# Gate/value products of a Strassen-Winograd feed-forward in another order

## The chip, the cores and the metric

The kernel runs on one core of a Trainium2 chip. The metric is device time in microseconds (us), the median of repeated executions. TensorE (PE) does the matrix products; VectorE (DVE), ScalarE (ACT) and GpSimd (POOL) do the arithmetic around them; SyncE (SP) and ScalarE issue DMA transfers. Each engine works through its own queue in order.

## The reference

One layer: a gated linear attention mixer, then a feed-forward with a causal convolution over three tokens, in fp32, for 2048 tokens of 1024 features. The part that the change touches is the first half of the feed-forward (FFN_DIM is 2816):

```python
def conv_ffn(h, w_up, conv_w, conv_b, w_down):
    u = causal_dwconv(h @ w_up, conv_w, conv_b)
    g, val = jnp.split(u, 2, axis=-1)
    return (jax.nn.silu(g) * val) @ w_down

x = x + y
h = rmsnorm(x, ffn_norm_w[i])
x = x + conv_ffn(h, ffn_w_up[i], ffn_conv_w[i], ffn_conv_b[i], ffn_w_down[i])
return rmsnorm(x, final_norm_w)
```

## The kernel before

Every large product is a 2x2 block product done with seven products in place of eight (Strassen-Winograd), named p1 to p7. Their operands are sums and differences of blocks: those of the weights are called `uw` here, those of the activations `h_s_p`. Every operand is split into a high and a low half, a cast on ScalarE and a difference on VectorE (`split`, L184 to L187), and each product adds three matmuls for each part (`mm3p`, L177 to L179).

The stages follow one another on TensorE: the mixer's products, the gate/value products (`phase_u`, from 893.7 us to about 1790 us of the span), and the down projection. Within `phase_u` the loops run over two token halves s of 1024 tokens ("passes"), eleven groups g in a pass, and fourteen jobs in a group: each of the seven products for the two tiles f = 2g and 2g + 1 (called f0 and f1 here; in the rows of the program's order, `uw_1_4_p5` is the weight operand of p5 for s = 1, f = 4). A job is twelve 128x512 matmuls into one PSUM bank. In the old order a group runs p1, p5, p6, p7, p4, p2, p3, each for f0 and then f1.

The banks carry partial sums from one product to the next:
- Bank `ua` takes p1, and is copied (c1); p6 is added, and it is copied (c2, L1219); p7 is added, and it is copied (c3, L1315); p4 is added, and it is copied into the tile u (L1322). All four copies are ScalarE's.
- Bank `uc` takes p5; VectorE adds c3 to it for one quarter of the output (L1318); then p3 is added, and VectorE adds c2 to it (L1328).
- Bank `ub` takes p2; VectorE adds c1 (L1310).

A product that adds into a bank waits until the bank's copy or add has been done. From the finished tiles u, `conv` does the convolution (an ACT pass at L1235, two DVE scalar-tensor-tensor passes at L1237, called STTs in the text, and the silu at L1239), and `gated` the product of gate and value (L1244) and the operand sums of the down projection on POOL (`as`, L1258 to L1262), which SyncE stores (L1248 to L1264).

`prep` makes the weight operands five jobs ahead of their products: raw weights are loaded by SyncE (`ur`, L1186), summed by POOL into `us` or in place (L1196 to L1214), and split. Two raw tiles per f are loaded in two parts. In the first pass the activation operands of the second pass are made beside the products, in 28 **operand steps** (`prep_h2`): VectorE takes a difference of two loaded blocks (L828), ScalarE and VectorE split it (`h2p`), and ScalarE's queue issues the store to `hd` (L823), a step late. A planner (`spread`, by estimated time) sets where each step falls in the program, one step per 11 us of its own estimate. `load_op` (L886) loads a 2 MB operand (four loads of 512 KB), three jobs behind its predecessor's last product, between the first pass and the second.

At the end of the gate/value stage `d_early` calls parts of the down projection's preparation, which uses freed slots of the operands.

Of the kernel before, what the change touches and what calls it, by code (L numbers as in the profile page):

```python
# [25 lines left out]
def hybrid_kernel(  # L26
# [45 lines left out]
    Y0, Y1, U0, U1 = 3.0, 2.8, 14.0, 11.0  # L72
# [709 lines left out]
    def blocks(tt, rws):  # L782

        for k in range(2):
# [4 lines left out]
            t = hb2_tile(f"hb2_{tt}_{k}") if tt < TT else cp_tile(f"hb3_{tt}_{k}")  # L789
# [12 lines left out]
    def prep_h2(jj, raw, pair):  # L802
# [13 lines left out]
        def store():  # L816
            while held:
                o, hl = held.pop(0)
                if s == 0:
                    nc.sync.dma_start(hd[s, o, j], f32(hl))  # L820
                else:
                    for i in range(2):
                        nc.scalar.dma_start(hd[s, o, j][:, i, :], f32(hl[i]))  # L823
# [58 lines left out]
    def load_op(s, o):  # L882

        t = uh.tile([P, 2, PAIRS, 512], F32R, tag=o, name=f"h_{s}_{o}", bufs=1)
        for j in range(PAIRS):
            nc.sync.dma_start(f32(t[:, :, j, :]), hd[s, o, j])  # L886
# [287 lines left out]
    def phase_u():  # L1174
        raws, wops, sums, made = {}, {}, {}, {}
        jobs = [(s, g, o, f) for s in range(NS) for g in range(NQ) for o in OPS for f in (2 * g, 2 * g + 1)]
        GJ = 2 * len(OPS)
# [39 lines left out]
        def copied(name, pa):  # L1217
            t = cp_tile(name)
            nc.scalar.copy(t, pa)  # L1219
            return t  # L1220
# [49 lines left out]
        bank = {}  # L1270
        for k, (s, g, o, f) in enumerate(jobs):
            if k % GJ in (2, 7) and k // GJ + 1 < NS * NQ:
                load(k // GJ + 1, int(k % GJ == 7))
            if k > 3:
                ls, lg, lo_, lf = jobs[k - 3]
                if ls + 1 < NS and lg == NQ - 1 and lf % 2 == 1:
                    need(*(f"h2p{jj}" for jj in range(PAIRS, 2 * PAIRS)))
                    load_op(ls + 1, lo_)
            if k == 6:
                while delayed:  # L1280
# [5 lines left out]
                spread(range(PAIRS, 2 * PAIRS), U0, U1, row_tile,  # L1286
                       lambda name: tuple(pools["us"].tile([P, 512], F32R, tag="as", name=f"{name}_{i}", bufs=AB) for i in range(2)))
# [6 lines left out]
            pairs = [((wh[:, kt * P:(kt + 1) * P], wl[:, kt * P:(kt + 1) * P]), (hop[o][0][:, kt], hop[o][1][:, kt])) for kt in range(HK)]  # L1294
            if o == "p1":
                a = bank["a", f] = mm_ps(f"ua_{s}_{f}")
                mm3p(a, pairs)
                made["p1", f] = copied(f"c1_{s}_{f}", a)
            elif o == "p5":
                c = bank["c", f] = aux_ps(f"uc_{s}_{f}")  # L1300
                mm3p(c, pairs)
            elif o == "p6":
                a = bank["a", f]
                mm3p(a, pairs, first=False, more=True)
                made["u2", f] = copied(f"c2_{s}_{f}", a)
            elif o == "p2":
                pb = mm_ps(f"ub_{s}_{f}")
                mm3p(pb, pairs)
                ev, _ = new_u(s, 0, f)
                nc.vector.tensor_add(ev, tiles1(pb), tiles1(made.pop(("p1", f))))  # L1310
            elif o == "p7":
                a = bank["a", f]
                mm3p(a, pairs, first=False, more=True)
                u3 = pools["us"].tile([P, 512], F32, tag="as", name=f"c3_{s}_{f}", bufs=AB)
                nc.scalar.copy(u3, a)  # L1315
                ev, od = new_u(s, 1, f)
                made["ev", f] = ev
                nc.vector.tensor_add(od, tiles1(bank["c", f]), tiles1(u3))  # L1318
            elif o == "p4":
# [3 lines left out]
                conv(s, 1, f)  # L1323
            else:
                c = bank.pop(("c", f))
                mm3p(c, pairs, first=False, more=True)
                _, od = tiles2(made["u", 0, f][:, 2:2 + TS])
                nc.vector.tensor_add(od, tiles1(c), tiles1(made.pop(("u2", f))))  # L1328
                conv(s, 0, f)
                gated(s, f)  # L1330
# [42 lines left out]
    def w_slots(o, q):  # L1373
        if q % 4 == 0:
            wgrp[o] = slots(("p7", "p4", "p3")[q // 4], f"dw_{o}_{q}")
        return wgrp[o][q % 4 * 2:][:2]

    def a_slots(k):
        if k % 4 == 0:
            wgrp["a"] = slots(("p6", "p2")[k // 4 % 2], f"da_{k}")  # L1380
# [31 lines left out]
    def d_early(o):  # L1412

        if o == "p6":
            load_chain()
        elif o == "p7":
            d_load(4)
        elif o == "p4":
            d_prep(2)
        elif o == "p3":  # L1420
# [77 lines left out]
    for n, (o, s) in enumerate(units):  # L1498
        banks = [(mm_ps if n % 2 == 0 else aux_ps)(f"pd_{o}_{s}_{m}") for m in range(PAIRS)]
# [54 lines left out]
```

## Time and profile before

| | |
|---|---|
| median of 3 runs | 2221.0 us (2214.37 to 2228.9) |
| profiled execution | 2224.22 us |
| its span | 2222.5 us |
| PE busy | 2122.4 us (95%) |
| DVE, ACT, POOL busy | 1636.5 (74%), 1107.9 (50%), 733.1 us (33%) |
| mean granted clock of TensorE | 0.986 |
| gate/value stage | 893.7 to about 1790 us |
| DMA | 411.78 MB, mean 185 GB/s |

The span runs from the first to the last instruction of one profiled execution. Busy time is summed per engine; a busy PE is not yet PE at its peak, since the clock that it is granted can fall. In rows of a timeline the first number is the start in us, the second the duration, and a bracket gives the idle time of the engine before it, with what ended it.

### The profile page before, as it was taken

How to read it: one execution, taken by the hardware profiler on the slowest of the kernel's cores; microseconds unless marked ns; L12 is line 12 of the kernel's file. 1: busy time of each engine (PE TensorE's matmuls, PEld its weight loads, DVE VectorE, ACT ScalarE, POOL GpSimd, SP SyncE). 2: the span in 40 equal slices, each digit the busy share in tenths (PEclk: the TensorE clock that was granted, in tenths of full speed). 3: DMA queues.
4: the chain of work that ended last, by engine and by line, in shares of the span. 5: the costliest groups of instructions: out<-in, count | busy, mean ns of one | idle time of the engine just before them, and what ended most of it. 6: DMA issues, size and time to landing. Idle time of an engine off the chain costs nothing.

```text
span 2222.5 us, 29090 instructions
## 1 busy us (share of the span) xinstructions
PE 2122.4 (95%) x9952; PEld 1743.6 (78%) x9952; DVE 1636.5 (74%) x2167; ACT 1107.9 (50%) x2024; POOL 733.1 (33%) x602
## 2 busy tenths in 40 slices
PE   6999999989998999898999999999999999999998
PEld 5888787877887787677887777788888887888886
DVE  8655787789778765488899786897877777457564
ACT  5554755565556676444555453454554443333342
POOL 1000011111111000355566664656555435036100
PEclk9999999999999999999999999999999999999999
DMA  6645684478557889935435348433332468354453
GB/s 210 218 165 182 203 264 157 131 223 299 164 161 235 283 321 352 315 117 174 155 120 193 105 139 288 142 112 102 103 111 85 159 243 289 128 180 152 142 176 113
DMA packets 305125, 411.78 MB, mean 185 GB/s; under 512 B 23742, under 2 KB 160110, under 8 KB 304976
## 3 DMA queue, kind: packets, MB, share of 16 engines
q1 hardware_dynamic: 267440, 346.99, 47.2%
q10 hardware_dynamic: 37536, 62.93, 8.4%
q8 instruction: 78, 1.28, 0.2%
q14 instruction: 71, 0.58, 0.1%
HBM read 266.70 MB, written 143.13 MB: 184 GB/s over the span
## 4 chain that ended last, share of the span: by engine, by line
PE 62%; DVE 14%; DMA 9%; issue 7%; ACT 3%; POOL 3%; SPq 1%; ACTq 0%; DVEq 0%; POOLq 0%
PE ua L177 5%; PE pd_p L178 5%; PE pd_p L179 5%; PE pd_p L177 5%; PE ua L179 5%; PE ua L178 5%; DVE t L1237 4%; PE uc L177 2%; PE uc L179 2%; PE uc L178 2%; PE mp_R L177 2%; PE mp_R L179 2%; PE mp_R L178 2%; PE mp_Y L177 2%; PE mp_Y L179 2%
## 5 line engine op out<-in xcount | busy, mean ns | idle before, releaser
L177 PE MATMUL ua<-h_p,uw_p 128*128 128x512 f32 x704 | 280.2, 398 | 23.6 <-ACT c L1219 23.6
L178 PE MATMUL ua<-h_p,uw_p 128*128 128x512 f32 x704 | 278.6, 396 | 0.0
L179 PE MATMUL ua<-h_p,uw_p 128*128 128x512 f32 x704 | 278.4, 395 | 0.0
L1237 DVE SCALAR_TENSOR_TENSOR t<-u,cw,t 128x1024 f32<-128x1024 f32 x176 | 263.3, 1500 | 8.9 <-ACT t L1235 7.9
L178 PE MATMUL pd_p<-dw_p,da 128*128 128x512 f32 x616 | 240.5, 390 | 3.1 <-DVE da L187 3.1
L179 PE MATMUL pd_p<-dw_p,da 128*128 128x512 f32 x616 | 240.1, 390 | 0.0
L177 PE MATMUL pd_p<-dw_p,da 128*128 128x512 f32 x616 | 240.1, 390 | 0.0
L187 DVE TENSOR_TENSOR uw_p<-ur,uw_p 128x512 fp32r<-128x512 f32 x176 | 168.3, 972 | 58.5 <-ACT uw_p L186 53.3
L187 DVE TENSOR_TENSOR da<-da_p,da 128x512 fp32r<-128x512 f32 x154 | 133.6, 920 | 105.4 <-ACT da L186 105.3
L186 ACT CAST da<-da_p 128x512 fp32r<-128x512 f32 x154 | 85.2, 619 | 208.9 <-PE pd_p L179 153.3
L177 PEld LDWEIGHTS ua<-h_p,uw_p 128*128 128x128 f32 x704 | 134.1, 191 | 57.2 <-ACT c L1219 27.6
L186 ACT CAST uw_p<-us 128x512 fp32r<-128x512 f32 x132 | 82.1, 622 | 165.8 <-POOL us L1199 108.3
L187 DVE TENSOR_TENSOR uw_p<-us,uw_p 128x512 fp32r<-128x512 f32 x132 | 120.4, 921 | 57.6 <-ACT uw_p L186 57.2
L179 PEld LDWEIGHTS ua<-h_p,uw_p 128*128 128x128 f32 x704 | 134.0, 190 | 30.1
L178 PEld LDWEIGHTS ua<-h_p,uw_p 128*128 128x128 f32 x704 | 134.3, 191 | 29.5
L177 PE MATMUL uc<-h_p,uw_p 128*128 128x512 f32 x352 | 138.3, 393 | 1.0 <-DVE t L1237 1.0
L179 PE MATMUL uc<-h_p,uw_p 128*128 128x512 f32 x352 | 138.0, 392 | 0.0
L178 PE MATMUL uc<-h_p,uw_p 128*128 128x512 f32 x352 | 138.0, 392 | 0.0
L178 PEld LDWEIGHTS pd_p<-dw_p,da 128*128 128x128 f32 x616 | 116.0, 188 | 28.0 <-DVE da L187 3.9
L1235 ACT ACTIVATE t<-u,cw 128x1024 f32<-128x1024 f32 x88 | 109.8, 1247 | 51.2 <-DVE u L1328 43.3
L179 PEld LDWEIGHTS pd_p<-dw_p,da 128*128 128x128 f32 x616 | 116.0, 188 | 24.2
L177 PEld LDWEIGHTS pd_p<-dw_p,da 128*128 128x128 f32 x616 | 115.9, 188 | 24.0
(269 smaller groups left out, 5476.2 us busy)
## 6 DMA issues: line engine op xcount, KB each, us to landing
ur<-in_ffn_w_up_dram SPq DMA_DIRECT2D x168, 256.0 KB, 3.7
da_p<-ad_p SPq DMA_DIRECT2D x154, 256.0 KB, 4.1
h_p<-hd_p SPq DMA_DIRECT2D x56, 512.0 KB, 8.1
ad_p<-as_p SPq DMA_DIRECT2D x88, 256.0 KB, 2.7
ad_p<-t SPq DMA_DIRECT2D x66, 256.0 KB, 3.5
x<-in_x_dram SPq DMA_DIRECT2D x32, 512.0 KB, 4.3
ch<-in_ffn_w_down_dram SPq DMA_DIRECT2D x61, 256.0 KB, 4.4
hr_A_p<-h1d_p SPq DMA_DIRECT2D x56, 256.0 KB, 2.7
```

Of the source, the lines that this page charges most:

```text
L177: nc.tensor.matmul(ps_ap, ah, bl, start=(first and i == 0), stop=False, **kw)
L178: nc.tensor.matmul(ps_ap, al, bh, start=False, stop=False, **kw)
L179: nc.tensor.matmul(ps_ap, ah, bh, start=False, stop=(last and i == len(pairs) - 1), **kw)
L186: nc.scalar.copy(hi, src)
L187: nc.vector.tensor_sub(lo, src, f32(hi))
L1235: nc.scalar.activation(t, u[:, 2:2 + TS], AF.Identity, scale=cw[:, 2, c:c + 1], bias=cw[:, 3, c:c + 1])
L1237: nc.vector.scalar_tensor_tensor(t, u[:, k:k + TS], cw[:, k, c:c + 1], t, op0=ALU.mult, op1=ALU.add)
```

## The change

The new order of a group is p1, p5, p6, p2 (each for f0 and f1), then p3 of f0, p7 of f0, p3 of f1, p7 of f1, p4 of f0, p4 of f1.

- Between p6 and p7 of one tile there stand now four or five products, before one.
- p5's bank is copied by ScalarE (c5) right after p5, and p7 is read by VectorE out of bank `ua`, which adds c5 (L1331), in place of the copy c3 and the add of c3 to `uc`. Then p4 is added into `ua`.
- p2 uses a bank of the same set as p5 and p3; the tiles of some copies change their pool.
- `conv` and `gated` of a tile are called one job later (`todo`, `late`).
- The operand steps fall at fixed jobs: at jobs 4, 6 and 8 (counted from 0) of the groups 1 to 10 of the first pass. Their stores are issued by SyncE.
- Raw weights of the next group are loaded at jobs 6 and 9, before at jobs 2 and 7.
- The loads of the second pass's operands follow the new order of products; those of p7 and p4 are issued by ScalarE, the others by SyncE.
- The last row tiles use another pool in an earlier stage, and the down projection takes its slots and banks from other operands.

```diff
-    Y0, Y1, U0, U1 = 3.0, 2.8, 14.0, 11.0
+    Y0, Y1 = 3.0, 2.8
+    H2AT = (4, 6, 8)
+    RAWAT = (6, 9)
...
-                        nc.scalar.dma_start(hd[s, o, j][:, i, :], f32(hl[i]))
+                        nc.sync.dma_start(hd[s, o, j][:, i, :], f32(hl[i]))
...
-        jobs = [(s, g, o, f) for s in range(NS) for g in range(NQ) for o in OPS for f in (2 * g, 2 * g + 1)]
-        GJ = 2 * len(OPS)
+        ORDER = [(o, i) for o in ("p1", "p5", "p6", "p2") for i in range(2)]
+        ORDER += [("p3", 0), ("p7", 0), ("p3", 1), ("p7", 1), ("p4", 0), ("p4", 1)]
+        jobs = [(s, g, o, 2 * g + i) for s in range(NS) for g in range(NQ) for o, i in ORDER]
+        GJ = len(ORDER)
...
-            if k % GJ in (2, 7) and k // GJ + 1 < NS * NQ:
-                load(k // GJ + 1, int(k % GJ == 7))
+            if h2u and k >= GJ and k % GJ in H2AT:
+                h2u.pop(0)()
+                while h2u and len(h2u) % 9 in (0, 1):
+                    h2u.pop(0)()
+            if k % GJ in RAWAT and k // GJ + 1 < NS * NQ:
+                load(k // GJ + 1, RAWAT.index(k % GJ))
...
-                    load_op(ls + 1, lo_)
+                    load_op(ls + 1, lo_, nc.scalar if lo_ in ("p7", "p4") else nc.sync)
...
             elif o == "p5":
                 c = bank["c", f] = aux_ps(f"uc_{s}_{f}")
                 mm3p(c, pairs)
+                made["p5", f] = copied(cp_tile(f"c5_{s}_{f}"), c)
             elif o == "p6":
                 a = bank["a", f]
                 mm3p(a, pairs, first=False, more=True)
-                made["u2", f] = copied(f"c2_{s}_{f}", a)
+                made["u2", f] = copied(out_tile(f"c2_{s}_{f}"), a)
             elif o == "p2":
-                pb = mm_ps(f"ub_{s}_{f}")
+                pb = aux_ps(f"ub_{s}_{f}")
...
+            elif o == "p3":
+                c = bank.pop(("c", f))
+                mm3p(c, pairs, first=False, more=True)
+                nc.vector.tensor_add(made.pop(("od", f)), tiles1(c), tiles1(made.pop(("u2", f))))
+                todo.append(lambda s=s, f=f: conv(s, 0, f))
             elif o == "p7":
                 a = bank["a", f]
                 mm3p(a, pairs, first=False, more=True)
-                u3 = pools["us"].tile([P, 512], F32, tag="as", name=f"c3_{s}_{f}", bufs=AB)
-                nc.scalar.copy(u3, a)
-                ev, od = new_u(s, 1, f)
-                made["ev", f] = ev
-                nc.vector.tensor_add(od, tiles1(bank["c", f]), tiles1(u3))
-            elif o == "p4":
+                made["ev", f], od = new_u(s, 1, f)
+                nc.vector.tensor_add(od, tiles1(a), tiles1(made.pop(("p5", f))))
+            else:
                 a = bank.pop(("a", f))
                 mm3p(a, pairs, first=False, more=True)
                 nc.scalar.copy(made.pop(("ev", f)), tiles1(a))
-                conv(s, 1, f)
-            else:
-                c = bank.pop(("c", f))
-                mm3p(c, pairs, first=False, more=True)
-                _, od = tiles2(made["u", 0, f][:, 2:2 + TS])
-                nc.vector.tensor_add(od, tiles1(c), tiles1(made.pop(("u2", f))))
-                conv(s, 0, f)
-                gated(s, f)
+                todo += [lambda s=s, f=f: conv(s, 1, f), lambda s=s, f=f: gated(s, f)]
+            for fn in late:
+                fn()
```

The change shifts line numbers: in the new kernel the split is at L188 and L189, the copies of p1, p5 and p6 at L1223, the adds of p2, p3 and p7 at L1321, L1325 and L1331, the STT at L1241.

ScalarE's queue around the copies c2, in the second group of the first pass, stands so before (`h2p` is an operand step's pair of halves, `hd` its place in memory):

```order
L186 CAST uw_0_2_p2_10133<-ur_0_2_1_9846 128x512
L186 CAST h2p_4_p5_0_10085<-h2r_4_0_9942 128x512
L823 DMA hd_1_p5_0_318<-h2p_4_p5_0_10085 128x512
L823 DMA hd_1_p5_0_318<-h2p_4_p5_1_10086 128x512
L1219 COPY c2_0_2_10131<-ua_0_2_10036 128x512
L186 CAST uw_0_3_p2_10150<-ur_0_3_1_9849 128x512
L186 CAST h2p_4_p7_0_10160<-h2r_4_1_9944 128x512
L823 DMA hd_1_p7_0_326<-h2p_4_p7_0_10160 128x512
L823 DMA hd_1_p7_0_326<-h2p_4_p7_1_10161 128x512
L1219 COPY c2_0_3_10148<-ua_0_3_10055 128x512
L186 CAST uw_0_2_p3_10181<-us_0_2_9933 128x512
L1315 COPY c3_0_2_10170<-ua_0_2_10036 128x512
```

and so in the changed kernel:

```order
L1223 COPY c5_0_2_10079<-uc_0_2_10066 128x512
L188 CAST uw_0_2_p7_10104<-ur_0_2_0_9806 128x512
L188 CAST h2p_4_p1_0_10099<-h2r_4_0_9819 128x512
L1223 COPY c5_0_3_10097<-uc_0_3_10084 128x512
L188 CAST uw_0_3_p3_10121<-us_0_3_9962 128x512
L188 CAST h2p_4_p5_0_10141<-h2r_4_0_9819 128x512
L1223 COPY c2_0_2_10119<-ua_0_2_10010 128x512
L188 CAST uw_0_3_p7_10152<-ur_0_3_0_9809 128x512
L188 CAST h2p_4_p7_0_10193<-h2r_4_1_9821 128x512
L1223 COPY c2_0_3_10138<-ua_0_3_10048 128x512
```

The casts of the steps stay between the copies; the stores are gone from this queue.

VectorE's queue around the adds, in the second group of the second pass (f = 2 is f0, f = 3 is f1; `u_1_24` and `u_1_25` are the value tiles of the two), stands so before, from the two p2 adds to the p3 adds:

```order
L1310 TENSOR_TENSOR u_1_2_13831<-ub_1_2_13818,c1_1_2_13635 128x4x128
L1237 SCALAR_TENSOR_TENSOR t_1_25_13811<-u_1_25_13772,cw_503,t_1_25_13811 128x1024
L1310 TENSOR_TENSOR u_1_3_13852<-ub_1_3_13839,c1_1_3_13654 128x4x128
L187 TENSOR_TENSOR uw_1_5_p5_13857<-us_1_5_13855,uw_1_5_p5_13857 128x512
L187 TENSOR_TENSOR uw_1_4_p6_13881<-us_1_4_13834,uw_1_4_p6_13881 128x512
L1328 TENSOR_TENSOR u_1_2_13831<-uc_1_2_13666,c2_1_2_13710 128x4x128
L187 TENSOR_TENSOR uw_1_5_p6_13919<-us_1_5_13855,uw_1_5_p6_13919 128x512
L1237 SCALAR_TENSOR_TENSOR t_1_2_13873<-u_1_2_13831,cw_503,t_1_2_13873 128x1024
L1328 TENSOR_TENSOR u_1_3_13852<-uc_1_3_13682,c2_1_3_13727 128x4x128
L1237 SCALAR_TENSOR_TENSOR t_1_2_13873<-u_1_2_13831,cw_503,t_1_2_13873 128x1024
```

and so in the changed kernel, from the p3 add of f0 to the p7 add of f1:

```order
L1325 TENSOR_TENSOR u_1_2_13749<-uc_1_2_13658,c2_1_2_13707 128x4x128
L189 TENSOR_TENSOR uw_1_5_p1_13816<-ur_1_5_0_13729,uw_1_5_p1_13816 128x512
L1241 SCALAR_TENSOR_TENSOR t_1_2_13811<-u_1_2_13749,cw_503,t_1_2_13811 128x1024
L1331 TENSOR_TENSOR u_1_24_13808<-ua_1_2_13603,c5_1_2_13671 128x4x128
L1241 SCALAR_TENSOR_TENSOR t_1_2_13811<-u_1_2_13749,cw_503,t_1_2_13811 128x1024
L189 TENSOR_TENSOR uw_1_4_p5_13834<-us_1_4_13832,uw_1_4_p5_13834 128x512
L1325 TENSOR_TENSOR u_1_3_13768<-uc_1_3_13676,c2_1_3_13724 128x4x128
L189 TENSOR_TENSOR uw_1_5_p5_13859<-us_1_5_13857,uw_1_5_p5_13859 128x512
L1241 SCALAR_TENSOR_TENSOR t_1_3_13852<-u_1_3_13768,cw_503,t_1_3_13852 128x1024
L1331 TENSOR_TENSOR u_1_25_13849<-ua_1_3_13640,c5_1_3_13689 128x4x128
L1241 SCALAR_TENSOR_TENSOR t_1_3_13852<-u_1_3_13768,cw_503,t_1_3_13852 128x1024
L189 TENSOR_TENSOR uw_1_4_p6_13876<-us_1_4_13832,uw_1_4_p6_13876 128x512
```

The two adds at L1331 read `ua`, the bank into which p4 is added next.

37 lines of the change are left out of this document (20 added, 17 removed).

## The prediction

> **What bounds the kernel now.** I began with the page's first part, to see which engine is full, and then cut the gate/value stage into its first pass over the tokens, the seam between the passes, and the second pass. The columns of the second fence are the stretch, its length, busy time and instructions of PE, PEld, DVE, ACT and POOL, the granted clock, the DMA share and GB/s.
>
> ```profile
> span 2222.5 us, 29090 instructions
> PE 2122.4 (95%) x9952; PEld 1743.6 (78%) x9952; DVE 1636.5 (74%) x2167; ACT 1107.9 (50%) x2024; POOL 733.1 (33%) x602
> ```
> ```profile
> 893.70:1357.10 463.40, 437.41 (x1865) 353.53 (x1864) 369.27 (x370) 225.46 (x353) 268.64 (x218) 0.98 0.53 170
> 1357.10:1404.40 47.30, 41.66 (x169) 33.20 (x168) 30.90 (x31) 18.66 (x28) 22.66 (x20) 0.93 0.80 264
> 1404.40:1790.00 385.60, 385.60 (x1681) 315.11 (x1680) 311.15 (x304) 194.92 (x293) 218.08 (x159) 1.00 0.38 117
> ```
>
> TensorE bounds the whole. In the second pass it has no idle time and a full clock: ten groups of fourteen products in 385.60 us, so 2.75 us for one product, and nothing there for any reordering to win. The first pass (eleven groups) and the seam (the second pass's first group) are 26.0 and 5.6 us idle, and below full clock besides. Next I asked who ends that idle time, with groups and waits.
>
> ```profile
> L177 PE MATMUL ua<-h_p,uw_p 128*128 128x512 f32 x704 | 280.2, 398 | 23.6 <-ACT c L1219 23.6
> L177 PE MATMUL ub<-h_p,uw_p 128*128 128x512 f32 x176 | 70.3, 399 | 4.6 <-issue 4.6
> PE ua L177 <- ACT c L1219: 23.6, 9, 5.0
> ```
>
> Nine waits of bank a, 23.6 us in all, end with the copy at L1219. A copy is 0.6 us, so its own wait is the thing to find. Here is ScalarE at the second and the seventh of these waits:
>
> ```profile
> 960.63 0.61 ACT L186 CAST h2p_p<-h2r 128x512 fp32r<-128x512 f32 x1
> 961.27 3.98 ACTq L823 DMA_DIRECT2D hd_p<-h2p_p  x2
> 965.29 0.59 ACT L1219 COPY c<-ua 128x512 f32<-128x512 f32 x1 [4.05 <-DVE h2p_p L187]
> ...
> 1251.47 0.62 ACT L186 CAST h2p_p<-h2r 128x512 fp32r<-128x512 f32 x1 [5.38 <-DMA hd_p<-h2p_p]
> 1251.99 0.58 ACT L1219 COPY c<-ua 128x512 f32<-128x512 f32 x1
> ```
>
> The copy c2 stands in ScalarE's queue behind an operand step: once behind the step's store, which waits for VectorE's half of the split, once behind a cast that waits for an earlier store to land. In the old order p7 needs the bank just one product after p6. The idle time also costs clock:
>
> ```profile
> 964.00:972.00 8.00, 6.07 (x15) 4.76 (x16) 5.52 (x5) 3.28 (x7) 3.62 (x3) 0.57 0.91 309
> 1006.00:1014.00 8.00, 5.50 (x24) 4.16 (x24) 4.28 (x6) 3.75 (x7) 3.47 (x3) 1.00 0.91 301
> 1048.00:1056.00 8.00, 4.63 (x16) 3.40 (x15) 6.77 (x7) 2.73 (x5) 3.58 (x3) 0.85 0.82 272
> 1250.00:1258.00 8.00, 5.38 (x13) 4.22 (x14) 2.04 (x3) 2.73 (x5) 2.13 (x2) 0.60 0.93 295
> 1386.00:1396.00 10.00, 6.67 (x18) 5.29 (x19) 4.17 (x5) 4.58 (x6) 0.26 (x1) 0.66 1.08 351
> ```
>
> After a shorter stop (1006) the clock stays at 1.00; at the longer ones it drops. Lost clock is (1 - clock) times the stretch: 3.4, 1.2 and 3.2 us at 964, 1048 and 1250, and 3.4 at the seam.
>
> **The change part by part.**
>
> *The waits on c2 go.* In the new order four products at least stand between p6 and p7 of one tile, about 11 us against the 5 us by which the copy is late, and the stores are off ScalarE. The first of the nine waits lies in the first group (below). The others are 23.6 - 4.8 = 18.8 us, and with the lost clock of 7.8 us the saving is **-26.6 us**. The cover is those four products; what comes late next is the copy of p7, now on VectorE.
>
> *The first group.* Its seventh job is p7 before and p2 after.
>
> ```profile
> 919.93 0.50 PE L177 MATMUL ua<-h_p,uw_p 128*128 128x512 f32 x1 [4.78 <-ACT c L1219]
> 905.30 15.11 SPq L886 DMA_DIRECT2D h_p<-hd_p  x9
> h_p<-hd_p SPq DMA_DIRECT2D x56, 512.0 KB, 8.1
> ```
>
> PE reached that job at 919.93 - 4.78 = 915.2. The operand loads still go out in the old product order. The nine issues from 905.30 are the last one of p4, four of p2 and four of p3, 1.68 us each; p2's last is the fifth, out at 913.7, landing 8.1 us later at 921.8. So the wait of 4.8 us becomes one of 6.6 us, which costs 1.8 us, and p3's loads (last out at 920.4, landed near 928.5) follow p2's two products so closely that another 1 or 2 us may show: **+3 us**, between +1 and +5.
>
> *The seam.* Two waits stand there, with SyncE's queue ahead of them:
>
> ```profile
> 1374.54 5.45 SPq L1264 DMA_DIRECT2D ad_p<-as_p  x4
> 1380.08 2.56 SPq L886 DMA_DIRECT2D h_p<-hd_p  x4
> ...
> 1389.33 0.76 PE L177 MATMUL ub<-h_p,uw_p 128*128 128x512 f32 x1 [4.61 <-issue]
> 1398.97 0.47 PE L177 MATMUL uc<-h_p,uw_p 128*128 128x512 f32 x1 [1.04 <-DVE t L1237]
> ```
>
> The load of p2's operand waited behind the stores of the sums, went out from 1380, and landed with 8.1 us per load only by 1389, when PE had stood for 4.6 us. With the clock (3.4) and the 1.0 us on p3 the seam loses 9.0 us. The new order loads p2 and p3 ahead of those stores and p7 and p4 on ScalarE's queue. I take **-6 us** of the 9: the DMA share there is already 1.08, and two queues draw on it. The ends are -9 and +3, the latter if p7's load is late by as much as p2's was.
>
> *The added wait.* p7's bank is now read by VectorE's add (L1331), with p4 of the same tile behind it. For f0 two products stand between; for f1 only p4 of f0, 2.75 us. Behind that add the queue holds STTs and weight halves, so p4 of f1 waits for all that is ahead of the add. No row shows this add, but the p3 add of f1 in the old order has the same work ahead of it (a weight half, then a convolution pass), and nothing of the product order waits for its bank:
>
> ```profile
> 1635.55 0.39 PE L179 MATMUL uc<-h_p,uw_p 128*128 128x512 f32 x1
> ...
> 1635.21 1.12 DVE L187 TENSOR_TENSOR uw_p<-us,uw_p 128x512 fp32r<-128x512 f32 x1 [1.25 <-ACT uw_p L186]
> 1636.37 2.43 DVE L1237 SCALAR_TENSOR_TENSOR t<-u,cw,t 128x1024 f32<-128x1024 f32 x1
> 1638.72 0.68 DVE L1328 TENSOR_TENSOR u<-uc,c 128x512 f32<-128x512 f32 x1
> ...
> 1636.41 1.30 POOL L1214 TENSOR_TENSOR us<-ur,us 128x512 f32<-128x512 f32 x1 [0.63 <-DVE uw_p L187]
> ```
>
> The product ends at 1635.94, the add ends at 1639.40, 3.46 us later, because the pass ahead of it took 2.43 us beside a POOL sum. Against 2.75 us that is 0.7 us of PE time. If the add came right behind its product it would be 0.7 us and cost nothing; if two POOL sums stood in its way, near 1.8. I take 0.7, the nearest row: eleven groups of the second pass, **+8 us** (0 to +20).
>
> The first pass has the operand steps on VectorE too, three to a group at fixed products:
>
> ```profile
> 1100.00:1141.00 41.00, 41.00 (x181) 33.40 (x180) 40.78 (x38) 22.04 (x34) 27.00 (x21) 1.00 0.49 160
> 1112.21 3.32 DVE L187 TENSOR_TENSOR uw_p<-us,uw_p 128x512 fp32r<-128x512 f32 x2
> L187 DVE TENSOR_TENSOR h2p_p<-h2r,h2p_p 128x512 fp32r<-128x512 f32 x28 | 34.4, 1231 | 6.4 <-POOL as_p L1262 2.7 <-ACT c L1219 2.6 <-DMA ad_p<-as_p 1.1
> L828 DVE TENSOR_TENSOR h2r<-h2r,h2r 128x512 f32<-128x512 f32 x16 | 21.3, 1329 | 0.3
> ```
>
> VectorE is busy 40.78 of 41.00 us there, so whatever is ahead of the add is late more often. Two halves that take 3.32 us together, or one step's half and difference (1.23 + 1.33 us), just ahead of it put 1 to 2.6 us on top of the second pass's 0.7. But the last step of a group is issued at the ninth job, three jobs ahead of p7 of f1, so I take 0.8 on top: 1.5 us in ten groups, **+15 us** (0 to +40).
>
> *No term.* c5 takes the place of c3 on ScalarE, copy for copy, 0.6 us each. ScalarE sheds the store issues; SyncE takes them. The deferred convolution is the same work one job later, covered by p4's two products. The last stage changes which banks and slots it uses, not its products.
>
> Sum against the profiled execution of 2224.2 us: -26.6 + 3 - 6 + 8 + 15 = -6.6, so **2217.6 us**; the median of the runs is 3 us lower than that execution, but they spread over 14 us, so I leave the number there, at 2217.
>
> **A rule weighed against the row.**
>
> ```profile
> 1137.92 0.68 DVE L187 TENSOR_TENSOR h2p_p<-h2r,h2p_p 128x512 fp32r<-128x512 f32 x1
> 1138.52 1.78 DVE L187 TENSOR_TENSOR uw_p<-ur,uw_p 128x512 fp32r<-128x512 f32 x1
> 1139.83 1.62 POOL L1202 TENSOR_TENSOR ur<-ur 128x512 f32<-128x512 f32 x1
> ```
>
> The same half takes 0.68 us and, beside POOL, 1.78: 1.1 us for each POOL sum in the way. The Trainium skill ("SBUF — State Buffer", section "Who interferes with whom") says that only the port pair which VectorE and GpSimd share causes contention, as an exclusive lock. By that rule the steps ahead of the new add come one sum apart from each other, and the change has put TensorE behind them; this speaks against the change, and it is rival C's mechanism. The trace agrees in kind, with the 1.78 against 0.68.
>
> **The rivals.**
>
> A, the forecast: the waits of ScalarE go, and a smaller one on VectorE takes their place in every group. 2217; by its own terms 2199 to 2240.
>
> B: the add mostly meets its 2.75 us. For it: before, the p7 copy was never waited for, some p3 adds came with no delay at all, and the new queue ahead of the add of f1 is one weight half and one pass, 0.68 + 1.27 us where POOL is quiet. With 0.1 us in the second pass and 0.4 in the first: -26.6 + 3 - 7 + 1 + 4 = -26, so 2198; with the whole seam (-9), a first group of +1 and no waits at all, 2190.
>
> C, slower: VectorE and POOL take turns through the window from p3 of f0 to p7 of f1. POOL's sums for the next group (two for p5, two for p7) start when the raw weights land, and the raw loads are now at the seventh and tenth job, so they land in this very window. It decides from the third sum ahead of the add: at 1.1 us each four sums give 4.4 us, of which some 0.4 fits into the time to spare, 4 us in each of ten groups of the first pass. There a stop this long also halves the clock (as at 1048), 1.2 us each in about seven groups. In the second pass, without the steps, 1.5 us in eleven. -26.6 + 4 - 3 + 40 + 8 + 17 = +39: 2263. Against it: POOL is busy just 218 of 385.6 us.
>
> The Trainium skill ("TensorE: Matmul & The Clock Gate", section "What's actually happening") gives an idle window of about 3.4 us after which the clock is halved; the rows fit, none lost in the stretch at 1006 and some at 1048.
>
> D: the change doesn't do what it says. The stores wait for VectorE in SyncE's queue now, with the raw loads and the stores of sums behind them; the 4 us that ScalarE stood at 961 would be stood by SyncE, raw weights come late, and the wait moves from the copy to the weight half of p5. Ten groups at 4 to 5 us in place of the 26.6 saved: about 2240 to 2250.
>
> **How the numbers follow.** A 0.48, B 0.29, C 0.17, D 0.06. A change of under 1% (2199 to 2243 around the median of 2221) can't be told from none here. A lies within it, B on the faster side by a hair (I count all of it there), C and D (in most of its reach) on the slower: faster 0.29, same 0.48, slower 0.23. The range takes in B's lower end and C's value: 2190 to 2264.
>
> **What would show it.** In the profile after, PE's wait on the copy of p6 should be gone and no ScalarE row should wait for an operand store. In its place PE's wait for bank a should be released by VectorE at L1331, near 8 us in the second pass and 15 in the first, always at p4 of f1. B is right if that row is under 5 us; C if it is over 40 and the clock in the first pass stays at 0.98 or below. The first group should wait at p2 to about 922, and the second pass's first group should take near 41 us in place of 47.3. I am wrong altogether if PE's new idle time is released by a DMA or by a weight half, or if the last stage, which I put at no change, moves by more than 3 us.

## The result, and the profile after

The changed kernel takes 2255.64 us in the median (2251.09 to 2257.07), against 2219.97 us before: ratio 1.0153, 95% interval [1.0116, 1.0191]. It is slower by 1.5%, where I had forecast no change.

The page of the kernel after, and the gate/value stage cut as in the prediction (first pass, seam, the ten groups behind it; columns as there):

```profile
span 2255.3 us, 28983 instructions
PE 2130.1 (94%) x9952; PEld 1745.2 (77%) x9952; DVE 1675.0 (74%) x2167; ACT 1112.3 (49%) x2024; POOL 754.0 (33%) x602
```
```profile
896.50:1371.80 475.30, 443.02 (x1865) 356.80 (x1864) 378.41 (x370) 227.81 (x352) 261.31 (x217) 0.96 0.52 166
1371.80:1424.40 52.60, 42.28 (x169) 32.32 (x168) 39.96 (x34) 22.15 (x33) 36.40 (x23) 0.94 0.72 238
1424.40:1827.40 403.00, 389.57 (x1682) 315.62 (x1681) 341.83 (x306) 194.19 (x288) 235.62 (x157) 1.00 0.38 114
```

Against 463.4, 47.3 and 385.6 us before, the three parts are 11.9, 5.3 and 17.4 us longer. The stage starts 2.8 us later, and what follows it takes 427.9 us in place of 432.5: +2.8 + 11.9 + 5.3 + 17.4 - 4.6 = 32.8, the whole difference of the spans. Groups and TensorE's waits after, with ScalarE's copies of bank a:

```profile
L179 PE MATMUL ua<-h_p,uw_p 128*128 128x512 f32 x704 | 285.0, 405 | 49.3 <-DVE u L1331 43.8 <-issue 2.4 <-ACT c L1223 1.7
PE ua L179 <- DVE u L1331: 43.8, 21, 5.3
PE ub L179 <- DMA h_p<-hd_p: 3.7, 1, 3.7
L1223 ACT COPY c<-ua 128x512 f32<-128x512 f32 x88 | 51.4, 584 | 69.2 <-PE ua L181 67.0 <-DVE uw_p L189 2.1
```

The waits on ScalarE's copy are gone: 1.7 us of 23.6 is left, and the copies now wait for products. In their place stand 43.8 us, 21 times, on the add of p7 (L1331): the wait that the prediction named, twice as large. Asked for the first pass alone, and then for the ten groups behind the seam, the waits read:

```profile
PE ua L179 <- DVE u L1331: 25.9, 11, 5.3
PE ua L179 <- DVE u L1331: 12.7, 9, 3.7
```

Here is the new bottleneck in the second pass (group from 1543.9), VectorE first, then POOL, then TensorE at p4 of f1:

```profile
1574.93 1.79 DVE L189 TENSOR_TENSOR uw_p<-us,uw_p 128x512 fp32r<-128x512 f32 x1
1576.64 0.68 DVE L1325 TENSOR_TENSOR u<-uc,c 128x512 f32<-128x512 f32 x1
1577.24 1.41 DVE L189 TENSOR_TENSOR uw_p<-us,uw_p 128x512 fp32r<-128x512 f32 x1
1578.63 1.28 DVE L1241 SCALAR_TENSOR_TENSOR t<-u,cw,t 128x1024 f32<-128x1024 f32 x1
1579.84 0.68 DVE L1331 TENSOR_TENSOR u<-ua,c 128x512 f32<-128x512 f32 x1
```
```profile
1568.69 1.30 POOL L1201 TENSOR_TENSOR us<-ur,ur 128x512 f32<-128x512 f32 x1 [7.68 <-DMA ur<-in_ffn_w_up_dram]
1571.65 2.27 POOL L1201 TENSOR_TENSOR us<-ur,ur 128x512 f32<-128x512 f32 x1
```
```profile
1580.67 0.47 PE L179 MATMUL ua<-h_p,uw_p 128*128 128x512 f32 x1 [0.85 <-DVE u L1331]
```

Ahead of the add stand p5's two weight halves (`us`), and they wait for POOL's sums, which wait for raw weights. SyncE shows why the raw weights are late. First before, with POOL's first sum of the group as its last row (group from 1597.2), then after (group from 1543.9); L1264 and L1268 store the sums of the down projection, L1252 a product of gate and value:

```profile
1602.67 0.92 SPq L1186 DMA_DIRECT2D ur<-in_ffn_w_up_dram  x2
1606.80 0.92 SPq L1186 DMA_DIRECT2D ur<-in_ffn_w_up_dram  x2
...
1610.27 5.11 SPq L1264 DMA_DIRECT2D ad_p<-as_p  x4
1615.47 2.10 SPq L1186 DMA_DIRECT2D ur<-in_ffn_w_up_dram  x4
...
1619.05 1.30 POOL L1196 TENSOR_TENSOR us<-ur,ur 128x512 f32<-128x512 f32 x1 [4.02 <-DMA ur<-in_ffn_w_up_dram]
```
```profile
1551.24 0.52 SPq L1252 DMA_DIRECT2D ad_p<-t  x1
...
1555.94 5.43 SPq L1268 DMA_DIRECT2D ad_p<-as_p  x4
1561.45 5.18 SPq L1191 DMA_DIRECT2D ur<-in_ffn_w_up_dram  x8
```
```profile
ur<-in_ffn_w_up_dram SPq DMA_DIRECT2D x168, 256.0 KB, 5.2
```

Before, the first raw part goes out 5.5 and 9.6 us into the group and only the second stands behind the stores of the sums, at 18.3; POOL starts p5's sum at 1619.05, 21.8 us in. After, both parts stand behind those stores: all eight loads go out in one row from 17.6 us on, they take 5.2 us to land in the median (3.7 before), and POOL starts 24.8 us in. At the loads themselves SyncE hardly waits any more: before, 401.7 us of its waits there in this stage ended with a weight half, which frees a slot of the raw weights; after, 7.4 us do. In the first pass the sum comes later still; there the operand steps' transfers stand in SyncE's queue as well (what they matter is tried below). This is the group from 1118.7, SyncE, POOL, VectorE, TensorE, and the clock there and in a group with a shorter wait:

```profile
1139.83 6.36 SPq L1191 DMA_DIRECT2D ur<-in_ffn_w_up_dram  x8
```
```profile
1148.26 2.35 POOL L1201 TENSOR_TENSOR us<-ur,ur 128x512 f32<-128x512 f32 x1 [11.57 <-DMA ur<-in_ffn_w_up_dram]
```
```profile
1155.36 1.21 DVE L189 TENSOR_TENSOR uw_p<-us,uw_p 128x512 fp32r<-128x512 f32 x1 [1.37 <-ACT uw_p L188]
1156.50 1.30 DVE L1241 SCALAR_TENSOR_TENSOR t<-u,cw,t 128x1024 f32<-128x1024 f32 x1
1157.73 0.68 DVE L1331 TENSOR_TENSOR u<-ua,c 128x512 f32<-128x512 f32 x1
```
```profile
1158.55 0.77 PE L179 MATMUL ua<-h_p,uw_p 128*128 128x512 f32 x1 [3.98 <-DVE u L1331]
```
```profile
1156.00:1164.00 8.00, 5.45 (x13) 4.33 (x14) 6.35 (x6) 4.25 (x6) 7.24 (x9) 0.59 0.01 2
1200.00:1208.00 8.00, 6.59 (x29) 5.45 (x30) 6.34 (x7) 6.03 (x9) 6.27 (x7) 1.00 0.00 1
```

The sum starts 29.6 us into the group, the add ends at 1158.4, the wait is 4 us, and the clock falls to 0.59 in that stretch, 3.3 us more.

### The profile page after: what moved, and what is told of

Same layout as the page of the kernel before. It is cut to its first block, busy times and chain, and to the rows that moved or that the text cites. A ratio compares the mean times of both kernels' runs of the same rounds, so it can differ in the third digit from the quotient of the medians.

```text
span 2255.3 us, 28983 instructions
## 1 busy us (share of the span) xinstructions
PE 2130.1 (94%) x9952; PEld 1745.2 (77%) x9952; DVE 1675.0 (74%) x2167; ACT 1112.3 (49%) x2024; POOL 754.0 (33%) x602
## 5 line engine op out<-in xcount | busy, mean ns | idle before, releaser
L179 PE MATMUL ua<-h_p,uw_p 128*128 128x512 f32 x704 | 285.0, 405 | 49.3 <-DVE u L1331 43.8
L1241 DVE SCALAR_TENSOR_TENSOR t<-u,cw,t 128x1024 f32<-128x1024 f32 x176 | 283.2, 1617 | 42.6 <-ACT t L1239 42.4
L180 PE MATMUL ua<-h_p,uw_p 128*128 128x512 f32 x704 | 282.3, 401 | 0.0
L181 PE MATMUL ua<-h_p,uw_p 128*128 128x512 f32 x704 | 281.6, 400 | 0.0
L189 DVE TENSOR_TENSOR da<-da_p,da 128x512 fp32r<-128x512 f32 x154 | 124.0, 856 | 122.7 <-ACT da L188 120.6
L179 PEld LDWEIGHTS ua<-h_p,uw_p 128*128 128x128 f32 x704 | 135.9, 193 | 90.2 <-issue 39.5
L189 DVE TENSOR_TENSOR uw_p<-us,uw_p 128x512 fp32r<-128x512 f32 x132 | 168.1, 1274 | 34.1 <-ACT uw_p L188 34.1
L188 ACT CAST da<-da_p 128x512 fp32r<-128x512 f32 x154 | 86.0, 620 | 215.0 <-PE pd_p L181 152.7
L189 DVE TENSOR_TENSOR uw_p<-ur,uw_p 128x512 fp32r<-128x512 f32 x176 | 157.9, 899 | 21.1 <-ACT uw_p L188 20.6
L188 ACT CAST uw_p<-ur 128x512 fp32r<-128x512 f32 x176 | 108.9, 624 | 126.3 <-PE ub L181 49.0
L181 PEld LDWEIGHTS ua<-h_p,uw_p 128*128 128x128 f32 x704 | 135.7, 193 | 31.8
L180 PEld LDWEIGHTS ua<-h_p,uw_p 128*128 128x128 f32 x704 | 135.8, 193 | 30.5
L1201 POOL TENSOR_TENSOR us<-ur,ur 128x512 f32<-128x512 f32 x44 | 72.2, 1641 | 209.4 <-DMA ur<-in_ffn_w_up_dram 176.5
L663 POOL TENSOR_TENSOR r<-r,gnw 128x512 f32<-128x512 f32 x32 | 48.1, 1503 | 266.7 <-ACT r L662 223.1
L188 ACT CAST uw_p<-us 128x512 fp32r<-128x512 f32 x132 | 81.5, 617 | 108.7 <-POOL us L1201 54.3
L180 PEld LDWEIGHTS pd_p<-dw_p,da 128*128 128x128 f32 x616 | 115.6, 188 | 25.1 <-DVE da L189 1.1
```

Source lines behind the costliest of these rows:

```text
L179: nc.tensor.matmul(ps_ap, ah, bl, start=(first and i == 0), stop=False, **kw)
L180: nc.tensor.matmul(ps_ap, al, bh, start=False, stop=False, **kw)
L181: nc.tensor.matmul(ps_ap, ah, bh, start=False, stop=(last and i == len(pairs) - 1), **kw)
L188: nc.scalar.copy(hi, src)
L189: nc.vector.tensor_sub(lo, src, f32(hi))
L663: nc.gpsimd.tensor_mul(r, r, sp["gnw"])
```

## The experiments

My theory after the result (theory 1): the loss is the late add, and it is late because POOL's sums for p5 and p7, fed by late raw weights, hold the queues ahead of it. The rivals: VectorE is simply too slow for a bank wanted one product later (theory 2), it is full and whatever comes last waits (3), the stores on SyncE (4), SyncE's queue as a whole (5).

**p7 copied by ScalarE.**

```diff
+                u3 = pools["us"].tile([P, 512], F32, tag="as", name=f"c7_{s}_{f}", bufs=AB)
+                nc.scalar.copy(u3, a)
-                nc.vector.tensor_add(od, tiles1(a), tiles1(made.pop(("p5", f))))
+                nc.vector.tensor_add(od, tiles1(u3), tiles1(made.pop(("p5", f))))
```

> One part undone: p7's bank is copied by ScalarE again (into a tile c7), and VectorE adds c7 and c5, so that p4 waits for a ScalarE copy and no longer for VectorE. Theory 1 (raw weights land late, POOL's sums for p5 and p7 run between p3 and p7, and every queue that handles p5's weight operand is held ahead of the add): the copy of f1 stands behind ScalarE's cast of p5's operand, which waits for the same POOL sum, but not behind VectorE's half and its convolution pass; it ends about 2.7 us behind its product in the second pass (wait near 0) and about 5.3 in the bad groups of the first pass (wait 2.5 in place of 4). The waits on p7's bank fall from 44 to 15 us, and with the clock the time to about 2220. Theory 2 (VectorE alone is too slow to read a bank that is wanted one product later; POOL and the loads have nothing to do with it): the waits go to nearly nothing, and with the clock that they cost the time to about 2195.

2271.46 us, ratio to before 1.0221 [1.0197, 1.0245]. Both expectations of the size were wrong: the waits did not fall. ScalarE around the copy of f1, and the wait:

```profile
1582.92 0.62 ACT L188 CAST uw_p<-us 128x512 fp32r<-128x512 f32 x1
1584.08 1.25 ACT L1239 ACTIVATE t<-u,cw 128x1024 f32<-128x1024 f32 x1 [0.53 <-DVE u L1325]
1585.23 0.56 ACT L1332 COPY c<-ua 128x512 f32<-128x512 f32 x1
```
```profile
PE ua L179 <- ACT c L1332: 53.5, 24, 6.8
```

The copy stands behind p5's cast and behind the convolution's first pass, which waits for the p3 add, which waits in VectorE's queue for p5's other half. Theory 2, as it was put, is out: without VectorE at the bank the wait is 53.5 us.

**p7 before p3**, three products of room.

```diff
-        ORDER += [("p3", 0), ("p7", 0), ("p3", 1), ("p7", 1), ("p4", 0), ("p4", 1)]
+        ORDER += [("p7", 0), ("p7", 1), ("p3", 0), ("p3", 1), ("p4", 0), ("p4", 1)]
```

> One size changed: the tail of a group runs p7 of f0, p7 of f1, p3 of f0, p3 of f1, p4 of f0, p4 of f1, so that three products (8.2 us) stand between p7 and p4 of one tile, not one or two; the down projection's early parts are called in the same new order. The adds were up to 6.0 us behind their products in the changed kernel, plus 0.7 us of their own, so both theories expect the waits on p7's bank (44 us, and some 20 us of half clock) to go, if the lateness itself stays as it is: about 2190 to 2200. If the lateness grows with the room (theory 3: VectorE is full in the first pass and whatever comes last waits), waits of more than 15 us come back at this or another bank, and the time stays above 2215. The copies c2 have three products in place of four and should not be waited for.

2267.4 us, 1.0201 [1.0174, 1.0228]; the waits on the add are 52.4 us, 36.0 of them in the first pass. Both theories had expected them to go. VectorE in a group of the first pass with a wait of 6.5 us, then in one of the second:

```profile
1248.30 1.25 DVE L189 TENSOR_TENSOR uw_p<-us,uw_p 128x512 fp32r<-128x512 f32 x1 [5.88 <-ACT uw_p L188]
...
1585.58 1.23 DVE L189 TENSOR_TENSOR uw_p<-us,uw_p 128x512 fp32r<-128x512 f32 x1 [2.49 <-ACT uw_p L188]
...
1592.67 0.68 DVE L189 TENSOR_TENSOR uw_p<-us,uw_p 128x512 fp32r<-128x512 f32 x1
1593.28 0.68 DVE L1331 TENSOR_TENSOR u<-ua,c 128x512 f32<-128x512 f32 x1
```

In the second group p7 of f1 ended near 1584.0, and the add comes 9 us later, again right behind p5's half of f1. The product moved forward by two, the add did not: it is tied to p5's half, not to its product. Distance alone buys nothing here. That is theory 3's outcome without its reason, since VectorE is not full: it stands idle for a cast of p5's operand, 2.49 us here and 5.88 us in the group of the first pass.

**Stores back on ScalarE.**

```diff
-                        nc.sync.dma_start(hd[s, o, j][:, i, :], f32(hl[i]))
+                        nc.scalar.dma_start(hd[s, o, j][:, i, :], f32(hl[i]))
```

> One part undone: the operand steps' stores are issued by ScalarE again, all else as changed. Theory 4 (the stores on SyncE hold the raw loads in the first pass; this makes its bad groups): the raw loads of the bad groups go out 2 us sooner, their sums and the add follow, the waits of the first pass fall from about 27 to 10 us and with the clock the time to about 2230. Theory 1 in its plain form (the raw loads are held by the slots of the raw weights and by the stores of the sums): the waits stay within 5 us of what they are, and a store that waits in ScalarE's queue adds a little, 2250 to 2265.

2259.85 us, 1.0171 [1.0148, 1.0195], with 46.9 us on the add, 28.5 of them in the first pass (25.9 in the changed kernel). Theory 4 falls.

**Without p5's and p7's sums.** POOL's sums for p5 and p7 are left out.

```diff
-                add(src, a21, a22)
+                src = a21
...
-                sub(src, src, a11)
+                sub(src, a22, a11)
...
-                sub(src, a11, a21)
```

> One suspected cost taken away: POOL's sums for the weight operands of p5 and p7 are left out (p5 and p7 use a raw block as it is, p6 starts from another block), all else as changed, so that p5's operand no longer waits for a second raw part nor for POOL. Theory 1: the add of p7 of f1 comes about 2 us behind its product as its queue is no longer held, the 44 us on p7's bank fall under 10, the clock comes back: about 2195. Theory 2: the waits stay near 1.3 us a group in the second pass, and the time above 2230.

2205.76 us, 0.9929 [0.9905, 0.9953]: 50 us under the changed kernel, and faster than before. The waits and the first pass:

```profile
PE ua L179 <- DVE u L1330: 11.3, 5, 3.6
```
```profile
900.60:1340.10 439.50, 429.21 (x1866) 348.85 (x1865) 354.54 (x372) 227.12 (x354) 198.27 (x174) 1.00 0.56 178
```

The first pass is 36 us shorter than after and its mean clock 1.00. This is the clearest result: same order, same banks, same add, and without these sums the add is mostly in time (five waits are left, where under 10 us had been expected).

**p5's sum from the first raw part.** The sum stays, but reads a11 in place of a22.

```diff
-                add(src, a21, a22)
+                add(src, a21, a11)
```

> The changed kernel, but p5's sum takes its second operand from the first raw part (a11 in place of a22), so that it no longer waits for the second part, which lands some 3 us later; POOL has as many sums of the same size. Theory 1a, in its part on late loads: p5's halves come about 3 us sooner, the waits on p7's bank fall from 44 to 10 to 20 us, the time to 2215 to 2230. Theory 1b (POOL's time, not its data): nothing changes by more than 8 us.

2232.59 us, 1.005 [1.0031, 1.0069].

```profile
PE ua L179 <- DVE u L1331: 28.4, 19, 4.3
```

With as many sums on POOL, the first of them 21.4 us into a group of the second pass in place of 24.8, 23 of the 50 us come back. So when the second part lands makes about half; the rest goes with the sums themselves, by POOL's time or the first part's landing, which no run separates.

**The add ahead in VectorE's queue.**

```diff
-                nc.vector.tensor_add(od, tiles1(a), tiles1(made.pop(("p5", f))))
+                added = nc.vector.tensor_add(od, tiles1(a), tiles1(made.pop(("p5", f)))).ins
...
+                with tc.issue_after(added) if added is not None else ExitStack():
                     prep(done)
...
+                with tc.issue_after(added) if added is not None else ExitStack():
                     fn()
```

> The changed kernel with one thing fixed in VectorE's queue: what is written after p7's add (the convolution of the tile before, the weight halves of later jobs) is also issued after it, so that for f1 only p5's half of f0 and the p3 add stand ahead of it, and p5's half of f1 behind. POOL's sums, the raw loads and the products stay. Theory 1a (the add is late because p5's half of f1, which waits for the second POOL sum, stands ahead of it in the queue): read off the changed kernel's trace the add would start at once in the second pass and some 2.2 us behind its product in the bad groups of the first; the waits on p7's bank fall from 44 to under 8 us, the clock comes back, and the time is 2195 to 2210. Theory 1b (POOL and VectorE slow each other throughout this window, whatever the order): waits of over 20 us stay, and the time is above 2230.

2287.46 us, 1.0288 [1.0256, 1.032], and 64.8 us on the add: the worst of all, against my expectation. ScalarE there:

```profile
1625.81 0.62 ACT L188 CAST uw_p<-ur 128x512 fp32r<-128x512 f32 x1 [6.75 <-DMA ur<-in_ffn_w_up_dram]
```

Moving work behind the add delays the gate, the down projection's sums and their stores, and behind those stores the next group's raw loads, so that now the casts of p1 wait for raw weights too. The lateness goes round from group to group; reading one turn of it from the trace had hidden that.

**Raw loads on ScalarE.**

```diff
-                    q = nc.scalar if s == 0 and g == 0 else nc.sync
+                    q = nc.scalar
```

> The changed kernel with all raw weight loads issued by ScalarE's queue, so that they no longer stand behind the stores of the sums and of the operand steps on SyncE. If SyncE's queue makes the raw loads late (theory 5), p5's sums come 2 us sooner in the second pass and up to 4 in the bad groups of the first, the waits on p7's bank fall from 44 to under 20 us, and the time to 2215 to 2230. If their slots do (the part that p5 needs is free only after p4's half, which is made when p4's weight buffer comes free, after the seventh product), the waits stay above 35 us; what ScalarE then waits for the slots may add to it, 2250 to 2270.

2259.32 us, 1.0159 [1.0135, 1.0182], 51.7 us on the add. Taking the raw loads out of SyncE's queue does not help, although in the changed kernel that queue does hold them (the rows above). On ScalarE's queue the second part goes out from 20.3 us into a group of the second pass, on SyncE's from 19.7, and p5's sum starts only about 1 us sooner. What holds the loads there is not shown: it may be their slots, since p7's and p4's halves now come last in a group and a slot is free only after them, or ScalarE's own queue.

**Steps at jobs 0, 1 and 2.**

```diff
-    H2AT = (4, 6, 8)
+    H2AT = (0, 1, 2)
```

> The changed kernel with the operand steps at jobs 0, 1 and 2 of a group in place of 4, 6 and 8. If the steps close ahead of the window are what makes the first pass wait more than the second (27 against 13 us, and the half clock), the waits of the first pass fall to about 13 us and the time to 2225 to 2235. If they are not (what makes it late are the sums and stores of the group before, which steps at jobs 0 to 2 delay still more), the waits stay or grow: 2250 to 2275.

2260.46 us, 1.0174 [1.0155, 1.0193], 48.8 us on the add, 30.5 of them in the first pass. The steps' place within a group is not what makes the first pass worse.

**Parts of the change in the kernel before.** The stores on SyncE alone:

```diff
-                        nc.scalar.dma_start(hd[s, o, j][:, i, :], f32(hl[i]))
+                        nc.sync.dma_start(hd[s, o, j][:, i, :], f32(hl[i]))
```

> The kernel before with one part of the change alone: the operand steps' stores are issued by SyncE. The waits on the copy c2 were of two kinds, behind a store in ScalarE's queue and behind an operand step's cast that waits for an earlier store to land. If the first kind carried most, the 23.6 us fall under 10 and the time to about 2200. If the casts carry it, the waits stay above 15 us and the time within 8 us of before.

2218.74 us, 0.9981 [0.9963, 0.9999]; 20.4 us of the 23.6 on c2 stay, so the casts carried most of them. Then p2 between p6 and p7 alone:

```diff
+        UORD = ("p1", "p5", "p6", "p2", "p7", "p4", "p3")
-        jobs = [(s, g, o, f) for s in range(NS) for g in range(NQ) for o in OPS for f in (2 * g, 2 * g + 1)]
+        jobs = [(s, g, o, f) for s in range(NS) for g in range(NQ) for o in UORD for f in (2 * g, 2 * g + 1)]
```

> The kernel before with the smallest form of the reordering alone: p2 moves between p6 and p7 (p1, p5, p6, p2, p7, p4, p3), so that c2 has three products of time; p7 is still copied by ScalarE, the loads, stores and operand steps stay. By my reading of the trace of before, the waits on c2 (23.6 us and some 10 of half clock) go, and nothing new is urgent, as the copy of p7 has no POOL-fed cast of p5 ahead of it: 2190 to 2200. If spacing by itself does not help, since a queue that is held somewhere comes late at the next bank (c3 ahead of p4), waits of over 10 us show at p4 or p3 and the time is above 2210.

2228.56 us, 1.0029 [1.0013, 1.0044]: c2 is no longer waited for, and the next bank is, against my reading of the trace.

```profile
PE uc L177 <- DVE u L1319: 30.3, 21, 8.2
```

With p5's bank copied by ScalarE besides (c5, and c2 in another pool):

```diff
+                made["p5", f] = copied(f"c5_{s}_{f}", c)
...
-                made["u2", f] = copied(f"c2_{s}_{f}", a)
+                t2 = made["u2", f] = out_tile(f"c2_{s}_{f}")
+                nc.scalar.copy(t2, a)
...
-                nc.vector.tensor_add(od, tiles1(bank["c", f]), tiles1(u3))
+                nc.vector.tensor_add(od, tiles1(made.pop(("p5", f))), tiles1(u3))
```

> The kernel before with p2 between p6 and p7 and, beyond that, p5's bank copied by ScalarE (c5), so that VectorE adds two copies and no product waits for a VectorE add; the loads, the stores on ScalarE, the operand steps and the convolution stay as before. Theory A (in any order the loss goes to that bank whose reader stands behind p5's weight half; take every bank's reader off VectorE and give it time, and nothing is left): the 30 us of waits at p3 of the run with p2 moved go, c2 and c3 are not waited for by over 5 us together, and the time is 2190 to 2200. Theory B (the first pass has too much work for VectorE and POOL, so weight operands themselves come late): PE waits of 15 us or more appear at casts or halves of weight operands, and the time is above 2210.

2284.97 us, 1.0274 [1.0251, 1.0297]. This one tests less than I meant. I had put c2 into the pool that holds the sums, and TensorE's wait (first row) is that of the copy for a slot (second row), which p3's half frees:

```profile
PE ua L177 <- ACT c L1308: 38.5, 20, 4.5
...
ACT c L1308 <- DVE uw_p L187: 81.7, 21, 6.2
```

With the stores on SyncE as well:

> The same with the operand steps' stores on SyncE. If ScalarE's queue still holds a copy behind a store at places, this gains another 2 to 5 us; if nothing waits for ScalarE any more, it is the same within 3 us; if SyncE then holds the raw loads, slower by 5 or more.

2278.2 us, 1.024 [1.0218, 1.0261]: 6.8 us less than without it, where 2 to 5 or nothing had been expected. It has the same flaw, so neither theory A nor B is decided by these two.

**The old order with steps at fixed jobs.** No reordering; the steps come where no urgent copy follows.

```diff
+            if h2u and k > 6 and k % GJ in (10, 11, 12):
+                h2u.pop(0)()
...
-                        nc.scalar.dma_start(hd[s, o, j][:, i, :], f32(hl[i]))
+                        nc.sync.dma_start(hd[s, o, j][:, i, :], f32(hl[i]))
...
-                    load_op(ls + 1, lo_)
+                    load_op(ls + 1, lo_, nc.scalar if lo_ in ("p2", "p3") else nc.sync)
```

> The kernel before in its old order of products, with the parts of the change around it: the operand steps at fixed jobs (10, 11 and 12 of each group of the first pass, where ScalarE has no copy that a product waits for), their stores on SyncE, and the operand loads of p2 and p3 for the second pass on ScalarE's queue. If the waits on c2 are just a matter of what stands ahead of the copy, they go (20 us and 8 of half clock) without any new urgent bank, and the seam loses some 5 of its 9 us: 2186 to 2196. If the steps, three in a row late in the group, hold VectorE and make p5's halves late instead, waits of over 10 us stay somewhere: 2205 to 2225.

2199.03 us, 0.9896 [0.9879, 0.9913]: faster than both kernels, but between the two expectations. Of the waits on c2 11.5 us are left, 5.8 in the first pass and 5.7 at the seam.

```profile
892.90:1327.40 434.50, 428.65 (x1865) 348.91 (x1864) 390.21 (x367) 223.80 (x351) 268.05 (x212) 1.00 0.54 176
1327.40:1374.90 47.50, 41.82 (x169) 33.40 (x168) 33.60 (x31) 20.16 (x31) 27.85 (x24) 0.93 0.87 301
1374.90:1760.70 385.80, 385.80 (x1682) 315.19 (x1682) 309.91 (x308) 194.53 (x292) 215.45 (x158) 1.00 0.38 117
```

The first pass is 434.5 us in place of 463.4, the second as it was. So the gain that the reorder was to bring could be had without it, by moving the steps; their stores on SyncE, also part of this run, gave about 2 us alone. The seam did not gain, 47.5 us against 47.3.

## Why the prediction was wrong, step by step

- **What bounds the kernel, and the waits that go:** right. The second pass had nothing to win, and the waits on c2 (23.6 us) went to 1.7. The 7.8 us of clock in the same term did not come back, as the first pass shows below.
- **The added wait, second pass:** right in place and engine, mis-sized. I took 0.7 us in eleven groups, 8 us. Nine waits in the ten groups behind the seam are 12.7 us (3.7 of them in the last group), the ten groups 17.4 us longer. The step that failed is the row I sized it by: the p3 add of before has one weight half ahead of it, and I called the work ahead of the new add the same. It has p5's half of f1 ahead, whose sum starts 3 us later into the group than before. I left the sum's start where the old kernel had it.
- **The added wait, first pass:** the largest miss. The terms make that pass 8.6 us shorter (-26.6 + 3 + 15); it is 11.9 us longer, 20.5 of the 39.4 us between forecast and measurement (-6.6 and +32.8). 15 us of waits was forecast with no half clock; measured are 25.9 us, and the clock lost in that pass, added up over the stretches in which it falls, is 17.1 us against 10.2 before, where the forecast left some 2. (I had read it slightly low before: the stretch at 1048 ends before the clock recovers, and 1.7 us are lost there, not 1.2.) My argument, that the last step is issued three jobs ahead and leaves only 0.8 us, looked at the steps; the runs with the stores and the steps moved show that they hardly matter, and the run without the sums shows what does.
- **The first group:** +3 was forecast. The wait at p2 is 3.7 us, not 6.6: TensorE came there at 920.6, and p2's operand landed near 924. The group is 49.7 us against 49.9.
- **The seam:** -6 was forecast, +5.3 came. The waits at p2 and p3 did go, but the new order put others there: 1.7 us at p6 behind a copy and 2.4 and 5.2 us at p4 of f0 and of f1.

```profile
1386.03 0.50 PE L179 MATMUL ua<-h_p,uw_p 128*128 128x512 f32 x1 [1.69 <-ACT c L1223]
1411.54 0.48 PE L179 MATMUL ua<-h_p,uw_p 128*128 128x512 f32 x1 [2.41 <-issue]
1419.74 0.76 PE L179 MATMUL ua<-h_p,uw_p 128*128 128x512 f32 x1 [5.17 <-DVE u L1331]
```

- **No term for the last stage:** the time after the gate/value stage is 4.6 us shorter, more than the 3 us that I had allowed. It can't be put down to the change: in the run with the stores alone on SyncE, whose last stage is the old one, it is 427.9 us as well. The 2.8 us by which the stage starts later are of the same kind; in kernels with the old earlier stages it starts between 892.9 and 898.7 us.
- **Rival C** had the mechanism and nearly the time (2263): POOL's sums in the window between p3 and p7, fed by raw loads that come late, and the clock. I gave it 0.17 with the argument that POOL is busy just 218 of 385.6 us. That was the wrong measure: in the changed kernel's gate/value stage POOL waits 171 us for raw weights at p5's sum (74 before), and then does four sums in a row where VectorE is wanted. That C's time came so near is partly luck: its terms make the first pass 25 us longer, where 11.9 were measured, and the seam 3 us shorter, where it became 5.3 longer. B and D did not happen; the run with the stores back on ScalarE speaks against D.
- **The rule weighed:** the Trainium skill ("SBUF — State Buffer", section "Who interferes with whom") names the port pair that VectorE and GpSimd share as the one place of contention, an exclusive lock. The trace agrees with single rows (a sum of 1.30 us takes 2.27 at 1571.65). But the run with p5's sum fed by the first raw part, with as many sums, shows that when they run is worth 23 us.
- **What stays open:** how the other half of the sums' 50 us divides between POOL's time and late data, and why every second group of the first pass is worse. The change also moved the raw loads from jobs 2 and 7 to 6 and 9; no run puts that back alone, so how much of their lateness comes from there is not known.

## What to carry to other kernels

Before moving a consumer away from its producer, ask what the move does to the loads that feed the work beside it: here both raw parts came to stand behind the same stores, and p5's sum started 3 us later in the group. In an in-order queue an instruction is as late as the latest thing ahead of it: with three products of room the add was still 9 us behind its product. Find what the instructions ahead wait for. And where a copy is late because of a bystander in its queue, try moving the bystander first.

## What the runs showed of the hardware

How easily the clock goes. After the stop of 3.98 us at 1158.55 the granted clock is 0.59 over 8 us, and the shorter wait in the stretch from 1200 leaves it at 1.00; the Trainium skill ("TensorE: Matmul & The Clock Gate", section "What's actually happening") gives a free-running window of about 3.4 us, and both rows fit it. Two stops of the changed kernel do not fit so plainly, one of 2.64 us at 1072.74, with a granted clock of 0.66 over the 10 us from 1070, and this one:

```profile
1327.21 0.48 PE L179 MATMUL ua<-h_p,uw_p 128*128 128x512 f32 x1 [2.10 <-DVE u L1331]
...
1326.00:1334.00 8.00, 6.79 (x23) 5.47 (x24) 6.34 (x7) 5.96 (x8) 6.24 (x8) 0.79 0.00 1
```

Here 2.10 us of idle time were enough to lose 1.7 us of clock, while a stop of 2.50 us in the kernel before (at 1009.89) left it at 1.00. So a stop that is safe in one group is not in another. And the raw loads of the changed kernel, mostly eight in a row, land 5.2 us after their issue in the median, against 3.7 us in the kernel before, where they go out in two parts.
